# Where the PSUM pools of the attention stage lie: projections' pool at the far end, scores' pool ahead of the others

## The chip, the cores and the metric

One core of a Trainium2 chip runs the whole layer as one program. TensorE (PE in the profile) multiplies, VectorE (DVE), ScalarE (ACT) and GpSimd (POOL) do the rest, SyncE (SP) issues most DMAs. Results of TensorE land in PSUM, which the program sees as eight banks, each 512 float32 wide on 128 partitions. The metric is the device time of one execution in microseconds, lower is better; the figure for a kernel is the median of its runs.

## The reference

One layer of a hybrid encoder: 2048 tokens, width 1024, everything in float32.

```python
h = rmsnorm(x, norm_mix_g)
proj = h @ w_in                                  # 1024 -> 512 (ssm) + 3 * 512 (q, k, v)
y_ssm = s5_mixer(u_ssm, ...)                     # diagonal complex scan, GELU, then y * sigmoid(y @ w_glu + b_glu)
y_att = chunked_attention(q, k, v, rel_bias)     # chunks of 64 frames, 8 chunks to the left, 8 heads of 64
mixed = concat([rmsnorm(y_ssm), rmsnorm(y_att)])
x = x + mixed @ w_out
h2 = rmsnorm(x)
x = x + (silu(h2 @ w_gate) * (h2 @ w_up)) @ w_down
return rmsnorm(x)
```

## The kernel before

Float32 accuracy comes from splits: an operand is cut into a high half that the multiplier takes as it is (a ScalarE copy to the type fp32r) and a low half, the rest (a VectorE subtraction); `split` at line 179 does both, and a product of two split operands is three matmuls (`mm3`, line 173): high by high, high by low, low by high.

The stages follow each other on TensorE: the SSM's input projection (`u_phase`), the attention over four blocks of 512 tokens with q, k and v projections and the SSM scan woven in (`att_phase`), the mixing (`mix_phase`: the gate of the SSM's output, two RMS norms, the output projection), then the feed-forward part (`gate_up_phase`, `down_phase`). The attention goes by 128 steps: at each step a generator per unit of work is advanced by so many pieces, and the matmuls are kept in the order in which the Python code emits them (`Ordered`, line 76). Semaphore waits are put in by the framework: the first instruction that writes a new tile waits until the last readers and writers of whatever lay in that memory are done, as far as an earlier wait on the same engine hasn't covered it.

PSUM is dealt out in pools, taken from a stack that grows from bank 0, or with `side="right"` from bank 7:

- `apf` (line 1856), two banks, for the whole of the attention: the tiles `pf`, into which the projections, the gate's first products and the small norm products go.
- `ups`, `ups2`, later `apro`: the banks of the stages ahead of the attention.
- `aps` (line 1036): the transposed probabilities `pt` (two banks) and two tiles `pj` of one bank (the probabilities times v, and products of the SSM).
- `aps2` (line 1037): the scores `sc`, two banks.
- After the attention all eight banks become one pool of four tiles `big` of two banks each (`pp`, line 1828). By the built program they are dealt in the order banks 0 and 1, 6 and 7, 4 and 5, 2 and 3, and round again.

The end of the attention overlaps the start of the mixing. `mix_phase` (line 1124) is a generator of which 17 pieces (`MIX_N`) run in the last steps of the attention: the gate of block 0 (its products in `pf` tiles), the loads and splits of block 1's gate operand (`load`, line 1324, tiles `w` of the pool `lp`, one high and one low half for each of four row groups), and then

```python
pb = bank()                                  # a pf tile
spread(k, te, pb, b.o[0], 0)                 # four transposes put the norm factors into pb
rstd2(b, 0, pb[:])                           # four VectorE products ya <- ya * gain * pb, line 1243
...
for n, _ in enumerate(glu(nxt, bk)):         # block 1's gate: four output tiles of 12 matmuls
    if n == R1:
        rstd1(b, 1, bk())
```

`bk` (line 1330) gives `pf` tiles as long as the attention lasts and `big` tiles after it. In this kernel all four output tiles of block 1's gate come after the attention, so the first of them is the first `big` tile. VectorE runs strictly in its own order there: the splits of `w`, the first product on `pb`, the gate's products on `raw` (line 1226), sums of squares (line 1163), and, between them, the other three products on `pb`.

Behind the gate stand the halves of the output projection that need the attention's part alone (`mixed(b, 0)`, `w_out`), the norm of the SSM's part, and the rest. The output weights of rows 0 to 511 were split during the attention (`out_weights`) and come back as halves by DMA (`woh`, `wol` from `wos`); the other half is split here.

## Time and profile before

| what | value |
|---|---|
| three runs | 2203.41, 2207.74, 2212.28 us |
| median | 2207.74 us |
| the profiled execution | 2205.35 us, of which the span from first to last instruction is 2203.6 us |
| granted TensorE clock, mean over the span | 0.996 |
| TensorE busy | 2146.7 us, 97% of the span |
| VectorE busy | 1534.4 us, 70% |
| ScalarE busy | 1005.5 us, 46% |
| DMA | 439.59 MB, 199 GB/s over the span |

The profile is one execution. In its rows a time is microseconds from the span's start, then how long the row lasted, the engine, the source line, the operation, the tile written and the tiles read, the shape and how many instructions the row merges. In brackets stands how long the engine had been idle ahead of it and what ended the idle time. "PEclk" and the clock columns give the granted share of TensorE's full clock. A line such as L83 is that of a helper through which all matmuls go; the tile names tell which stage a row belongs to.

### The profile page before, as it was taken

Reading aid. Unit: us, or ns where it says so; the run is one execution under the profiler, and the core shown is the slowest. Engines: PE = TensorE matmul, PEld = TensorE weight load, DVE = VectorE, ACT = ScalarE, POOL = GpSimd, SP = SyncE. Lnnn points to the kernel's source line nnn. Section 1 sums busy time; section 2 is a strip of 40 time slices with the busy share of each in tenths; the row PEclk is TensorE's granted clock in tenths of the full one; section 3 lists DMA queues with packets and bytes.
Section 4 is the critical chain, followed back from the end, with each engine's and each line's share of the span. In section 5 each row is a group of like instructions: output and inputs, shape, how many; then the busy total and the mean of one; then the engine's idle time right before and its main releaser. Section 6 shows DMA issues by size and latency. Waiting matters only on the chain.

```text
span 2203.6 us, 30105 instructions
## 1 busy us (share of the span) xinstructions
PE 2146.7 (97%) x10606; PEld 1810.2 (82%) x10606; DVE 1534.4 (70%) x2671; ACT 1005.5 (46%) x1686; POOL 374.1 (17%) x839
## 2 busy tenths in 40 slices
PE   8999999999998999999999999999999999999998
PEld 7787898898886888788888887888888787888887
DVE  8767566665566667767766768766665577689785
ACT  6356566565576521633333344333333443354332
POOL 3367777676210000000000000000000100000000
PEclk9999999999999999999999999999999999999999
DMA  9788978966644347736555558555332495465552
GB/s 334 233 286 272 300 229 265 295 191 189 206 132 158 124 146 231 253 105 196 167 168 201 200 184 283 173 174 194 105 124 91 136 379 187 159 222 196 194 217 77
DMA packets 197879, 439.59 MB, mean 199 GB/s; under 512 B 20128, under 2 KB 37584, under 8 KB 190624
## 3 DMA queue, kind: packets, MB, share of 16 engines
q1 hardware_dynamic: 189904, 412.44, 56.1%
q0 software_dynamic: 7824, 25.24, 3.7%
q8 instruction: 83, 1.36, 0.2%
q14 instruction: 68, 0.56, 0.1%
HBM read 294.20 MB, written 135.29 MB: 195 GB/s over the span
## 4 chain that ended last, share of the span: by engine, by line
PE 80%; DVE 6%; DMA 5%; POOL 4%; issue 3%; ACT 2%; SPq 0%; DVEq 0%; ACTq 0%; POOLq 0%
PE X L83 21%; PE ps L83 20%; PE Y L83 11%; PE pf L83 8%; PE big L83 7%; PE W L83 5%; PE pj L83 3%; PE pt L86 2%; PE sc L83 2%; DVE lo L181 1%; POOL X L646 1%; POOL st L643 1%; POOL X L645 1%; DMA x<-xt 1%; POOL st L644 1%
## 5 line engine op out<-in xcount | busy, mean ns | idle before, releaser
L83 PE MATMUL X<-hi,c 128*128 128x512 f32 x1408 | 451.3, 391 | 7.7 <-DVE c L181 7.0
L83 PE MATMUL ps<-hd,hd 128*128 128x512 f32 (+1 forms) x1920 | 428.7, 384 | 3.8 <-DVE hd L181 2.0
L83 PEld LDWEIGHTS ps<-hd,hd 128*128 128x128 f32 x1920 | 353.2, 188 | 75.5 <-DVE hd L181 2.7
L83 PEld LDWEIGHTS X<-hi,c 128*128 128x128 f32 x1408 | 265.5, 189 | 64.1 <-DVE c L181 7.8
L83 PE MATMUL X<-lo,c 128*128 128x512 f32 x704 | 275.1, 391 | 0.0
L181 ACT CAST hd<-hd 128x1536 fp32r<-128x1536 f32 (+1 forms) x106 | 147.6, 1394 | 232.0 <-DMA hd<-hq 167.7
L83 PE MATMUL Y<-hi,c 128*128 128x512 f32 x704 | 225.0, 390 | 1.5 <-DVE u L1562 1.5
L181 DVE TENSOR_TENSOR hd<-hd 128x1536 fp32r<-128x1536 f32 (+1 forms) x106 | 174.1, 1644 | 37.3 <-ACT hd L181 36.5
L181 DVE TENSOR_TENSOR c<-S,c 128x512 fp32r<-128x512 f32 x176 | 121.0, 688 | 101.7 <-ACT c L181 101.5
L1666 POOL DMA_DIRECT2D hd<-hq x7 | 5.2, 747 | 1065.2 <-PE X L83 1053.0
L1558 ACT COPY u<-X 128x512 f32<-128x512 f32 x132 | 77.5, 588 | 198.4 <-PE X L83 198.4
L181 ACT CAST c<-S 128x512 fp32r<-128x512 f32 x176 | 109.5, 622 | 122.9 <-PE Y L83 61.8
L83 PE MATMUL big<-m,woh 128*128 128x512 f32 x512 | 158.9, 391 | 0.0
L1700 DVE TENSOR_TENSOR acc<-acc,ps 128x512 f32<-128x512 f32 x196 | 130.2, 682 | 39.4 <-PE ps L83 39.2
L83 PEld LDWEIGHTS Y<-hi,c 128*128 128x128 f32 x704 | 133.0, 189 | 29.7 <-DVE u L1562 1.9
L83 PEld LDWEIGHTS X<-lo,c 128*128 128x128 f32 x704 | 132.8, 189 | 27.5
L181 ACT CAST c<-raw 128x512 fp32r<-128x512 f32 x132 | 82.3, 623 | 147.8 <-PE Y L83 71.2
L83 PE MATMUL pf<-hi,w 128*128 128x512 f32 x416 | 147.4, 407 | 0.0
L83 PE MATMUL Y<-lo,c 128*128 128x512 f32 x352 | 137.4, 390 | 0.0
L980 DVE TENSOR_TENSOR ptl<-pt,pth 128x640 fp32r<-128x640 f32 (+3 forms) x152 | 98.1, 646 | 43.8 <-ACT pth L979 39.8
L979 ACT CAST pth<-pt 128x640 fp32r<-128x640 f32 (+3 forms) x152 | 83.8, 551 | 79.9 <-PE pt L86 74.3
L963 ACT ACTIVATE s<-s,mn 128x640 f32<-128x640 f32 (+4 forms) x128 | 98.0, 765 | 46.5 <-DVE mn L960 43.5
(486 smaller groups left out, 4258.1 us busy)
## 6 DMA issues: line engine op xcount, KB each, us to landing
w<-wss SPq DMA_DIRECT2D x36, 1024.0 KB, 6.5
hq<-g SPq DMA_DIRECT2D x140, 256.0 KB, 2.1
hd<-hq SPq DMA_DIRECT2D x35, 768.0 KB, 4.4
hd<-wc SPq DMA_DIRECT2D x35, 768.0 KB, 5.9
raw<-in_w_gate SPq DMA_DIRECT2D x44, 512.0 KB, 3.7
raw<-in_w_up SPq DMA_DIRECT2D x44, 512.0 KB, 4.1
wc<-px SPq DMA_DIRECT2D x66, 256.0 KB, 3.2
wss<-w SPq DMA_DIRECT2D x12, 1024.0 KB, 6.4
```

The lines of the kernel that those rows point to most:

```text
L83: return self.tc.keep_in_program_order(self.tc.nc.tensor.matmul(*a, **b))
L86: return self.tc.keep_in_program_order(self.tc.nc.tensor.transpose(*a, **b))
L181: return nc.scalar.copy(hi, raw), nc.vector.tensor_tensor(lo, raw, f32(hi), op=ALU.subtract)
L643: eng.tensor_tensor(t[:, :, :, :n], src, ar, op=ALU.mult)
L644: eng.tensor_tensor(t2[:, :, :, :n], src[:, ::-1], aw, op=ALU.mult)
L645: eng.tensor_tensor(dst, dst, t[:, :, :, :n], op=ALU.add)
L646: eng.tensor_tensor(dst, dst, t2[:, :, :, :n], op=ALU.add)
L963: nc.scalar.activation(s[:, :nk], s[:, :nk], AF.Exp, bias=mn[:], scale=-1.0, accum_out=sums[sb, pr][:, hh, qp : qp + 1])
L979: nc.scalar.copy(pth[:, a:b, qp, :], pt[:, a:b, :])
L980: k.low = nc.vector.tensor_tensor(ptl[:, a:b, qp, :], pt[:, a:b, :], f32(pth[:, a:b, qp, :]), op=ALU.subtract).ins
L1558: nc.scalar.copy(u[:], ps[:])
L1700: V.tensor_tensor(a, a, ps[:], op=ALU.add)
```

## The change

Two edits. The pools `aps` and `aps2` are opened in the other order, and `apf` is taken from the right-hand end.

```diff
@@ -1033,8 +1033,8 @@
         nbt = S["nba"], k.t(aa, "nbb", [P, 640])
         bias_corners(k, nbt[1])
         sp = tc.alloc_tile_pool(name="ssm", reuse_waits="tile", bufs=1)
+        psum2 = cx.enter_context(tc.tile_pool(name="aps2", bufs=1, space=bass.MemoryType.PSUM, reuse_waits="tile"))
         psum = cx.enter_context(tc.tile_pool(name="aps", bufs=1, space=bass.MemoryType.PSUM, reuse_waits="tile"))
-        psum2 = cx.enter_context(tc.tile_pool(name="aps2", bufs=1, space=bass.MemoryType.PSUM, reuse_waits="tile"))
         units = []
@@ -1853,7 +1853,7 @@
-            with tc.tile_pool(name="apf", bufs=2, space=bass.MemoryType.PSUM, reuse_waits="tile") as k.pfs:
+            with tc.tile_pool(name="apf", bufs=2, space=bass.MemoryType.PSUM, reuse_waits="tile", side="right") as k.pfs:
```

In the built program the banks are then these:

| pool and tile | banks before | banks now |
|---|---|---|
| `apf`: `pf` | 0, 1 | 6, 7 |
| `aps2`: `sc` | 6-7 | 0-1 |
| `aps`: `pt` | 2-3 | 2-3 |
| `aps`: `pj` | 4, 5 | 4, 5 |
| `ups`: `ps` | 2 to 5 | 0 to 3 |
| `ups2`: `pp` | 6, 7 | 4, 5 |
| `big`, in the order dealt | 0-1, 6-7, 4-5, 2-3 | 0-1, 6-7, 4-5, 2-3 |

No instruction is added, removed or moved on any engine; what differs is waits on TensorE. The first is at the first score tile of the attention, whose wait for earlier matmuls names an earlier one of them (transposes into the pool `apro`). The second is on TensorE at the end of the attention, at the first `big` tile (`big_8444`, first output tile of block 1's gate; `w` is the gate operand, `hi`, `lo`, `xt` the gate's weights; a name in square brackets is the semaphore waited for, that of VectorE or of TensorE itself):

```order
-L83 MATMUL big_8444<-w_7913,hi_1467_6615 128x512 [waits DVE_49,PE_49]
 L83 MATMUL big_8444<-w_7913,hi_1467_6615 128x512
+L83 MATMUL big_8444<-w_7913,hi_1467_6615 128x512 [waits DVE_49]
 L83 MATMUL big_8444<-w_7913,lo_1468_6616 128x512
-L83 MATMUL big_8444<-w_7913,hi_1516_6847 128x512 x2
+L83 MATMUL big_8444<-w_7913,hi_1516_6847 128x512
+L83 MATMUL big_8444<-w_7913,hi_1516_6847 128x512 [waits DVE_49]
```

The tile's first matmul waits for nothing now; its second, which reads the low half of the operand, waits for the split of that half, and so does every third matmul after it. Before, the first matmul waited for the fourth product on `pb` (`pb` lay in the same banks) and needed no wait of its own for the splits, which stand ahead of that product on VectorE. The same wait stands now on TensorE twelve matmuls later, at the second `big` tile (`big_8460`, second output tile of the same gate), which lies on banks 6 and 7:

```order
-L83 MATMUL big_8460<-w_7913,hi_1467_6615 128x512 x2
+L83 MATMUL big_8460<-w_7913,hi_1467_6615 128x512 [waits DVE_49,PE_49]
+L83 MATMUL big_8460<-w_7913,hi_1467_6615 128x512
 L83 MATMUL big_8460<-w_7913,lo_1468_6616 128x512
 L83 MATMUL big_8460<-w_7913,hi_1516_6847 128x512 x2
```

Everything behind it, on all engines, waits for what it waited for before.

## The prediction

> **What bounds the kernel now.** I read the page's head and its chain of waits first.

> ```profile
> span 2203.6 us, 30105 instructions
> PE 2146.7 (97%) x10606; PEld 1810.2 (82%) x10606; DVE 1534.4 (70%) x2671; ACT 1005.5 (46%) x1686; POOL 374.1 (17%) x839
> PE 80%; DVE 6%; DMA 5%; POOL 4%; issue 3%; ACT 2%; SPq 0%; DVEq 0%; ACTq 0%; POOLq 0%
> ```

> TensorE is busy 97% of the span and holds 80% of the chain that ended last. An edit of waits can pay only where TensorE stands still: 2203.6 − 2146.7 = 57 us in all. So next the waits of TensorE by the instruction waited for (total us, times, longest).

> ```profile
> PE pt L86 <- DVE ptl L980: 13.8, 18, 2.2
> PE X L83 <- DVE c L181: 7.0, 2, 3.5
> PE big L83 <- DVE ya L1243: 6.3, 1, 6.3
> ```

> The third line is the place of the change: one single wait of 6.3 us, for the products on `pb` at line 1243. TensorE's timeline around it:

> ```profile
> 673.00 0.62 PE L86 MATMUL pj<-ident,rb 128*128 128x128 f32 x4
> 679.96 1.19 PE L83 MATMUL big<-w,hi 128*128 128x512 f32 x2 [6.34 <-DVE ya L1243]
> 685.21 0.76 PE L83 MATMUL big<-w,hi 128*128 128x512 f32 x2
> 688.08 0.62 PE L83 MATMUL big<-w,hi 128*128 128x512 f32 x2
> 690.13 0.94 PE L83 MATMUL big<-ones,sq 128*128 128x1 f32 x8
> ```

> The last work of the attention ends at 673.62. The gate's first output tile starts at 679.96, its second at 685.21, its third at 688.08. Twelve matmuls take 685.21 − 679.96 = 5.25 us the first time; nine of the third tile take 690.13 − 688.08 = 2.05, so twelve are 2.73 us at their full pace. The first tile ran slowly, and the views by windows (columns: length, busy time and count of PE, PEld, DVE, ACT, POOL, then the granted clock, DMA share, GB/s) say why:

> ```profile
> 678.00:679.00 1.00, 0.00 (x0) 0.00 (x0) 1.00 (x2) 0.74 (x2) 0.00 (x0) 0.83 1.03 315
> 683.00:685.00 2.00, 2.00 (x6) 1.53 (x5) 0.73 (x2) 0.00 (x0) 0.00 (x0) 0.50 1.03 420
> 685.00:686.00 1.00, 1.00 (x4) 0.81 (x4) 0.00 (x0) 0.50 (x1) 0.00 (x0) 0.76 1.03 422
> ```

> The granted clock falls to half inside the gap (0.83 over 678 to 679: from about 678.66) and returns at about 685.48 (0.76 over 685 to 686). So the wait costs its 6.34 us and some 2.6 us of slow matmuls behind it.

> **The change, part by part.** The first edit that can show is at the first score tile, whose wait for earlier transposes now names an earlier one.

> ```profile
> 126.33 0.30 PE L83 MATMUL sc<-hi2x,hi0x 128*128 128x128 f32 x1
> ```

> That row has no idle time ahead of it, so nothing stood there to be saved, and an earlier event can't be later: 0.

> The second is the `big` tiles. The first one now lies where the scores lay; its own waits are the splits of `w`. VectorE's and ScalarE's rows:

> ```profile
> 670.47 2.49 DVE L181 TENSOR_TENSOR w<-w,w 128x512 fp32r<-128x512 f32 x4
> 679.07 0.74 DVE L1243 SCALAR_TENSOR_TENSOR ya<-ya,ga,pf 128x512 f32<-128x512 f32 x1
> 681.24 2.49 DVE L181 TENSOR_TENSOR m<-ya,m 128x512 fp32r<-128x512 f32 x4
> 679.84 0.62 ACT L181 CAST m<-ya 128x512 fp32r<-128x512 f32 x1 [0.64 <-DVE ya L1243]
> 685.50 0.69 ACT L1229 ACTIVATE sg<-big,bg 128x512 f32<-128x512 f32 x1 [5.04 <-PE big L83]
> 686.22 0.69 DVE L1230 TENSOR_TENSOR w<-w,sg 128x512 f32<-128x512 f32 x1 [2.50 <-ACT sg L1229]
> ```

> The four splits end at 672.96, ahead of 673.62, so the first tile runs at once: twelve matmuls, still at the full clock (it fell only at 678.66), 673.62 + 2.73 = 676.35. The second tile lies under `pb` and waits for the fourth product, which VectorE ends at 679.07 + 0.74 = 679.81. Nothing that VectorE does between 670.47 and there reads what TensorE writes after 673.62, so that time stays, and the second tile starts at 679.96, where the first one did. The gap shrinks from 6.34 to 679.96 − 676.35 = 3.61 us.

> What that is worth depends on the pace of the second tile. Before, 24 matmuls took 688.08 − 679.96 = 8.12 us from the end of the wait; now twelve are left. At full pace they take 2.73 us: gain 8.12 − 2.73 = 5.39. At the pace of the first tile before, 5.25: gain 2.87. Which one is read from the other two gaps of this length:

> ```profile
> 908.58 1.22 PE L83 MATMUL X<-hi,c 128*128 128x512 f32 x2 [3.51 <-DVE c L181]
> 907.00:908.00 1.00, 0.00 (x0) 0.00 (x0) 1.00 (x3) 0.00 (x0) 0.00 (x0) 0.67 1.01 391
> 914.00:915.00 1.00, 1.00 (x6) 0.82 (x5) 0.62 (x1) 1.00 (x3) 0.00 (x0) 0.91 1.24 377
> 1349.88 0.73 PE L83 MATMUL X<-hi,c 128*128 128x512 f32 x2 [3.46 <-DVE c L181]
> 1350.00:1352.00 2.00, 2.00 (x7) 1.58 (x8) 2.00 (x4) 0.00 (x0) 0.00 (x0) 0.77 0.00 0
> 1352.00:1354.00 2.00, 2.00 (x6) 1.56 (x5) 0.84 (x2) 0.44 (x1) 0.00 (x0) 0.50 0.64 217
> 1354.00:1355.00 1.00, 1.00 (x4) 0.79 (x4) 0.00 (x0) 0.67 (x2) 0.00 (x0) 0.76 0.83 311
> ```

> After an idle stretch of 3.51 us the clock was halved from about 907.34 to 914.18, which cost half of the 5.6 us that TensorE worked in it: 2.8 us. After 3.46 us it was halved for 0.92 + 2.00 + 0.48 = 3.4 us, from about 1351.1: 1.7 us lost. Both gaps are a little shorter than the 3.61 us to come, and both brought the clock down, so I take a fall. By a long fall the gain is 2.87, by a short one 8.12 − (2.73 + 1.7) = 3.69. Two of the three falls seen (678.66, 907.34) were long: (2 × 2.87 + 3.69) / 3 = 3.1 us.

> [...]

> **Does the gain reach the end?** Behind the second tile every wait must be met about 3 us sooner. ScalarE's sigmoid of the first tile can run at 680.46 (behind its cast at 679.84) in place of 685.50, and VectorE's product with it behind its `m` splits, at 681.24 + 2.49 = 683.73; both engines stood idle there for lack of the first tile (5.04 and 2.50 us), so their queues move up too. On TensorE the whole stretch behind is full, except for short waits for the norm's first step (`nv`) of 0.8 us in all:

> ```profile
> 690.00:735.00 45.00, 44.74 (x216) 37.45 (x215) 29.28 (x79) 21.99 (x33) 0.00 (x0) 1.00 0.43 142
> 735.00:780.00 45.00, 44.75 (x212) 37.40 (x212) 26.43 (x62) 28.30 (x38) 0.00 (x0) 1.00 0.39 127
> 850.00:910.00 60.00, 56.49 (x252) 46.52 (x251) 44.13 (x78) 23.16 (x37) 0.00 (x0) 0.98 0.80 261
> PE big L83 <- DVE nv L112: 0.8, 3, 0.3
> 709.39 1.28 ACT L1196 ACT_TABLE_LOAD   x1
> 710.69 4.20 ACT L1196 ACTIVATE raw<-yr 128x512 f32<-128x512 f32 x4
> L1175 SPq DMA_DIRECT2D yr<-y x4: 462/1088/3620, 690.0 to 694.8; - x4
> DMA to landing us min/median/max: 6.4/7.0/8.8
> ```

> Of the transfers, the one that doesn't hang on TensorE is `yr`: issued up to 694.8 and landed at the latest by 694.8 + 8.8 = 703.6 for a GELU that starts at 710.69. It has 7 us to spare. SyncE issues it behind loads that wait for the output weights' splits, which move up as well; even unmoved it would do. So I carry 3.1 us to the end: 2205.35 − 3.1 = 2202.2 for an execution like the profiled one. The three runs have their median 2.4 us above it, so I state 2207.74 − 3.1 = **2204.6 us**.

> **The rivals.**
> *The clock holds* through the shorter gap: 5.39 us, 2207.74 − 5.4 = 2202.3. [...] Against it: both gaps near 3.5 us fell. [...]

> *The gain is lost behind.* Between 850 and 910 TensorE waits once for 3.5 us, at 908.58, at the end of a chain of transfers, with DMA busy 0.80 of the time. If these are paced by the queues and not by TensorE, TensorE gets there 3 us sooner and waits 6.6: time 2207.7. Against it: that stretch's loads and stores are released by results of the output projection, which move with TensorE.

> *The banks themselves cost time.* The scores are now read from banks 0 and 1, next to the transposes in 2 and 3, and the projections go to 6 and 7. If reading or writing there were slower, the place is the score step:

> ```profile
> L960 DVE CUSTOM_DVE_ANT_0 s<-sc,nbb 128x640 f32<-128x640 f32 (+2 forms) x64 | 47.3, 739 | 39.5 <-PE sc L83 37.7 <-POOL st L643 1.2
> L83 PE MATMUL X<-lo,c 128*128 128x512 f32 x704 | 275.1, 391 | 0.0
> L83 PE MATMUL Y<-lo,c 128*128 128x512 f32 x352 | 137.4, 390 | 0.0
> L83 PE MATMUL W<-lo,c 128*128 128x512 f32 x176 | 68.5, 389 | 0.0
> ```

> The attention has 128 such steps; 0.1 us more on each, all of it exposed, is 12.8 us: 2207.7 − 3.1 + 12.8 = 2217.4. It outweighs the gain from 0.024 us a step on. Against it: in the built program `W` lies on banks 0 and 1, `X` on 2 to 4, `Y` on 5 to 7, and the same matmul takes 389, 391 and 390 ns.

> *Nothing changes* because the first tile waits for something that the profile hides behind the late product: 2207.7. I count it with the lost gain; the order of waits leaves only the splits, which end by 672.96.

> **How the numbers follow.** The forecast, clock fallen, gain kept: 0.6. Clock holds: 0.15. Gain lost or absent: 0.15. Banks slower: 0.1, by all sizes. A change under 0.5% (11 us) can't be told from none by measuring this kernel. The first three cases lie at 2202 to 2208, all inside it; only the slow-bank case crosses it upward, half of the time: slower 0.05. Faster by over 0.5% needs the full 5.4 us and another 5.6 from the spread of the runs (4.5 us on either side of the median): 0.04. Same: 0.91. The range takes the cases' ends, 2202.3 and 2207.7, and for the scatter of a median of few runs such as those shown about 4 us below and 3 above: 2198 to 2211.

> **What would show it.** In the changed profile TensorE's first `big` row should stand directly behind the last `pj` row with no idle time, last about 2.7 us for twelve matmuls, and be followed by one gap of 3.6 us ended by `ya` L1243; the second tile should run at a granted clock of 0.5 and the third start 2.9 to 3.7 us sooner after the end of the attention. The stretch from there to 850 should be as full as before, and the wait at `X` near 905 still about 3.5 us. A gap of 6 us at the first tile would say that the wait wasn't the one named; a longer wait at `X` would say that the gain was lost; longer L960 rows or fuller idle time in the attention would say that the banks matter.

## The result, and the profile after

The change ran 22 times beside 22 runs of the kernel before: median 2207.44 us (2199.93 to 2211.37) against 2210.88 (2203.41 to 2218.30). The ratio is 0.9981, 95% interval 0.9973 to 0.9989: 2210.88 × 0.0019 = 4.2 us faster, 2.4 to 6.0. Forecast were 3.1 us and 2204.6 us. The time lies 2.8 us above that because the kernel before, run 19 times more, has its median 3.1 us above the three runs shown; by size and sign the difference is as forecast. The prediction held that a change under 11 us can't be told from none; with 22 runs on each side 4.2 us can.

The waits of TensorE in the changed kernel (total us, times, longest), three lines of the list:

```profile
PE X L83 <- DVE c L181: 6.5, 2, 3.4
PE big L83 <- DVE ya L1243: 3.6, 1, 3.6
PE pj L83 <- DMA Bst<-bsts: 2.5, 1, 2.5
```

The wait at `big` went from 6.3 to 3.6 us. TensorE's timeline at the place, end of the attention to third tile of the gate:

```profile
680.80 0.62 PE L86 MATMUL pj<-ident,rb 128*128 128x128 f32 x4
681.18 0.71 PE L83 MATMUL big<-w,hi 128*128 128x512 f32 x2
...
683.32 0.84 PE L83 MATMUL big<-w,xt 128*128 128x512 f32 x3
687.78 0.70 PE L83 MATMUL big<-w,hi 128*128 128x512 f32 x2 [3.62 <-DVE ya L1243]
...
692.19 0.63 PE L83 MATMUL big<-w,hi 128*128 128x512 f32 x2
```

The first tile stands directly behind the attention, without idle time; the wait now stands ahead of the second. From the end of the attention (680.80 + 0.62 = 681.42) the third tile starts 692.19 − 681.42 = 10.77 us later; before it was 688.08 − 673.62 = 14.46. That is 3.69 us. VectorE and ScalarE there:

```profile
678.30 2.49 DVE L181 TENSOR_TENSOR w<-w,w 128x512 fp32r<-128x512 f32 x4
686.89 0.75 DVE L1243 SCALAR_TENSOR_TENSOR ya<-ya,ga,pf 128x512 f32<-128x512 f32 x1
688.32 0.69 ACT L1229 ACTIVATE sg<-big,bg 128x512 f32<-128x512 f32 x1
```

The fourth product ends at 687.64, 6.22 us after the end of the attention, as before (679.81 − 673.62 = 6.19). The first sigmoid runs as soon as ScalarE is free, 6.90 us after that end in place of 11.88. The clock behind the gap, by windows (granted clock is the third number from the right):

```profile
688.00:689.00 1.00, 1.00 (x5) 0.77 (x5) 0.90 (x2) 0.97 (x3) 0.00 (x0) 0.84 1.05 418
689.00:692.00 3.00, 3.00 (x9) 2.32 (x8) 3.00 (x6) 1.89 (x3) 0.59 (x1) 0.50 1.02 408
692.00:693.00 1.00, 1.00 (x6) 0.82 (x5) 1.00 (x2) 0.81 (x2) 0.00 (x0) 0.96 1.06 426
```

It was halved for 0.32 + 3.0 + 0.08 = 3.4 us: a short fall, 1.7 us lost, and by the prediction's own sum 8.12 − (2.73 + 1.7) = 3.69 us gained.

The profiled execution itself is longer than that of before, 2209.6 against 2203.6 us, and that has nothing to do with the place: the attention ended 7.8 us later (681.42 against 673.62). The third wait above, for a transfer at 202.04, is one part of it, 2.5 us. Slow clock at two other places is another:

```profile
260.00:267.00 7.00, 6.00 (x25) 5.26 (x26) 1.51 (x2) 4.48 (x11) 4.13 (x9) 0.76 1.00 395
507.00:515.00 8.00, 6.29 (x20) 5.38 (x21) 4.23 (x8) 2.54 (x5) 5.75 (x8) 0.57 0.90 257
```

At half the clock these cost up to 7 × (1 − 0.76) = 1.7 and 8 × (1 − 0.57) = 3.4 us. The kernel before shows a scatter of that size without the change: the mean granted clock is 0.989 to 0.996 in its five profiles and 0.993 here. Two single spans can't be compared to a few microseconds here. The distance between two landmarks around the place can, and the ratio over many runs.

### The profile page after: what moved, and what is told of

It reads as the page before. It is cut to its first block, busy times and chain, and to the rows that moved or that the text cites. A ratio compares the mean times of both kernels' runs of the same rounds, so it can differ in the third digit from the quotient of the medians.

```text
span 2209.6 us, 30105 instructions
## 1 busy us (share of the span) xinstructions
PE 2153.8 (97%) x10606; PEld 1815.0 (82%) x10606; DVE 1535.5 (69%) x2671; ACT 1004.9 (45%) x1686; POOL 372.7 (17%) x839
## 4 chain that ended last, share of the span: by engine, by line
PE 80%; DVE 6%; DMA 5%; POOL 4%; issue 3%; ACT 2%; SPq 0%; DVEq 0%; ACTq 0%; POOLq 0%
PE ps L83 21%; PE X L83 20%; PE Y L83 10%; PE pf L83 8%; PE big L83 7%; PE W L83 5%; PE pj L83 3%; PE pt L86 2%; PE sc L83 2%; DMA lo<-hc 1%; DVE lo L181 1%; POOL X L646 1%; DMA x<-xt 1%; POOL X L645 1%; DMA raw<-in_w_out 1%
## 5 line engine op out<-in xcount | busy, mean ns | idle before, releaser
L83 PE MATMUL X<-hi,c 128*128 128x512 f32 x1408 | 450.6, 391 | 7.2 <-DVE c L181 6.5
L83 PE MATMUL ps<-hd,hd 128*128 128x512 f32 (+1 forms) x1920 | 430.1, 385 | 2.0 <-DVE hd L181 2.0
L83 PEld LDWEIGHTS ps<-hd,hd 128*128 128x128 f32 x1920 | 354.4, 189 | 74.0 <-DVE hd L181 2.7
L83 PEld LDWEIGHTS X<-hi,c 128*128 128x128 f32 x1408 | 265.1, 188 | 63.5 <-DVE c L181 7.3
L83 PE MATMUL X<-lo,c 128*128 128x512 f32 x704 | 274.6, 390 | 0.0
L181 ACT CAST hd<-hd 128x1536 fp32r<-128x1536 f32 (+1 forms) x106 | 147.5, 1394 | 232.3 <-DMA hd<-hq 166.8
L83 PE MATMUL Y<-hi,c 128*128 128x512 f32 x704 | 225.1, 390 | 1.9 <-DVE u L1562 1.5
L181 DVE TENSOR_TENSOR hd<-hd 128x1536 fp32r<-128x1536 f32 (+1 forms) x106 | 174.2, 1644 | 37.0 <-ACT hd L181 36.5
L181 DVE TENSOR_TENSOR c<-S,c 128x512 fp32r<-128x512 f32 x176 | 121.0, 688 | 100.7 <-ACT c L181 100.5
L181 ACT CAST c<-S 128x512 fp32r<-128x512 f32 x176 | 109.5, 622 | 122.0 <-PE Y L83 62.1
L83 PE MATMUL big<-m,woh 128*128 128x512 f32 x512 | 161.2, 396 | 0.0
L83 PEld LDWEIGHTS Y<-hi,c 128*128 128x128 f32 x704 | 132.5, 188 | 30.6 <-DVE u L1562 2.4
L83 PEld LDWEIGHTS X<-lo,c 128*128 128x128 f32 x704 | 132.6, 188 | 27.6
L181 ACT CAST c<-raw 128x512 fp32r<-128x512 f32 x132 | 82.2, 623 | 147.7 <-PE Y L83 70.7
L83 PE MATMUL pf<-hi,w 128*128 128x512 f32 x416 | 148.8, 410 | 0.0
L83 PE MATMUL Y<-lo,c 128*128 128x512 f32 x352 | 137.2, 390 | 0.0
L980 DVE TENSOR_TENSOR ptl<-pt,pth 128x640 fp32r<-128x640 f32 (+3 forms) x152 | 98.1, 646 | 43.9 <-ACT pth L979 39.8
```

Source lines behind the costliest of these rows:

```text
L83: return self.tc.keep_in_program_order(self.tc.nc.tensor.matmul(*a, **b))
L181: return nc.scalar.copy(hi, raw), nc.vector.tensor_tensor(lo, raw, f32(hi), op=ALU.subtract)
L980: k.low = nc.vector.tensor_tensor(ptl[:, a:b, qp, :], pt[:, a:b, :], f32(pth[:, a:b, qp, :]), op=ALU.subtract).ins
```

## The experiments

Twelve runs followed, of eight kernels: the kernel before and the change again, and six others. The table gives for each the distance from the end of the attention to the start of the gate's third tile and to the four transposes of the SSM norm (`big<-ident,no`, the last landmark ahead of the norm's product), from one profile each, and the ratio to the kernel before with its interval. The kernel before has five profiles; its distances to the third tile were 14.46, 14.57, 14.79, 13.66 and 13.96 us, mean 14.29, and to the transposes 31.74, 31.85, 32.07, 30.93 and 31.24 us, mean 31.57.

| kernel | third tile, us | transposes, us | ratio | interval |
|---|---|---|---|---|
| before | 14.46 | 31.74 | 1 | |
| the change | 10.77 | 28.09 | 0.9981 | 0.9973 to 0.9989 |
| the change again | 10.69 | 28.07 | 0.9987 | 0.9976 to 0.9998 |
| far end only | 10.77 | 28.09 | 0.9988 | 0.9977 to 0.9999 |
| scores first only | 13.27 | 30.55 | 1.0000 | 0.9988 to 1.0013 |
| first tile twice | 9.16 | 26.43 | 0.9974 | 0.9962 to 0.9986 |
| products early, far end | 5.32 | 24.48 | 0.9973 | 0.9961 to 0.9984 |
| products early, old banks | 9.28 | 26.56 | 0.9962 | 0.9946 to 0.9977 |
| first tile eight times | 24.36 | 41.64 | 1.0048 | 1.0031 to 1.0064 |

**One edit at a time.** Far end only:

```diff
-            with tc.tile_pool(name="apf", bufs=2, space=bass.MemoryType.PSUM, reuse_waits="tile") as k.pfs:
+            with tc.tile_pool(name="apf", bufs=2, space=bass.MemoryType.PSUM, reuse_waits="tile", side="right") as k.pfs:
```

> Only the pool pf goes to the far end; the transposes pt then lie on banks 0-1, pj on 2 and 3, the scores on 4-5. Theory (a wait of TensorE for the late product on pb, and the clock behind it): the first big tile lies under pt, long read, so it starts at once as in the change, and the second waits for the product. From the end of the attention's last matmul to the start of the gate's third tile 9.1 us if the clock holds, 10.8 after a short fall, 11.6 after a long one (14.5 before); ratio to before about 0.998, between 0.9975 and 0.9988. Rival (the place of the scores' banks carries part of the gain): less than that, nearer to 1.000.

Scores first only is the other half of the diff, `aps2` opened ahead of `aps`.

> Only the scores' pool is opened first: sc on banks 2-3, pt on 4-5, pj on 6 and 7, pf stays on 0 and 1. Theory: the first big tile still lies under pf, TensorE waits 6.3 us there for the product at line 1243, 14.5 us to the third tile; ratio 1.000, within 0.001. Rival (banks have a speed of their own): three pools of the attention have moved, so the score and transpose rows get longer or shorter and the ratio leaves 1.000 by more than 0.001.

In TensorE's timelines, the far end alone has the changed kernel's picture, a first tile at once and 3.6 us ahead of the second:

```profile
676.17 0.62 PE L86 MATMUL pj<-ident,rb 128*128 128x128 f32 x4
676.55 0.71 PE L83 MATMUL big<-w,hi 128*128 128x512 f32 x2
683.14 0.70 PE L83 MATMUL big<-w,hi 128*128 128x512 f32 x2 [3.59 <-DVE ya L1243]
687.56 0.63 PE L83 MATMUL big<-w,hi 128*128 128x512 f32 x2
```

and the scores' order alone has that of before:

```profile
675.48 0.62 PE L86 MATMUL pj<-ident,rb 128*128 128x128 f32 x4
682.46 1.19 PE L83 MATMUL big<-w,hi 128*128 128x512 f32 x2 [6.35 <-DVE ya L1243]
```

So the edit on `apf` is the change; opening the scores' pool first adds nothing that these runs can tell. That its third tile comes at 13.27 us, ahead of all five profiles of before, lies in the clock: it came back 9.3 us after the end of the attention, in those five 10.1 to 12.5 us after it. The kernel with the scores first alone moves the scores, the transposed probabilities and `pj` to other banks and its time is the same, 1.0000. The score rows of the changed kernel, in the list of costliest groups, are as long as before (739 ns):

```profile
L960 DVE CUSTOM_DVE_ANT_0 s<-sc,nbb 128x640 f32<-128x640 f32 (+2 forms) x64 | 47.3, 739 | 42.4 <-PE sc L83 41.8
```

The rival that the banks have a speed of their own is out for these three pools, to within the interval of 0.0012. For the banks of the change itself the traces say the same: its attention, with the kernels built on it, ends at 674.8 to 681.4 us in four profiles, that of the kernel before at 673.6 to 679.7 in five.

**The clock behind the gap.** The second pass over the first tile fills most of the gap with work:

```diff
-                for q in range(4):
-                    mm3(te, ps[:, :512], Wg[q][0][:, cs], Wg[q][1][:, cs], *gate_operand(k, q), q == 0, q == 3)
+                for q in range(8 if f == 0 and twice else 4):
+                    mm3(te, ps[:, :512], Wg[q % 4][0][:, cs], Wg[q % 4][1][:, cs], *gate_operand(k, q % 4), q % 4 == 0, q % 4 == 3)
```

> The change, and the first output tile of block 1's gate is computed twice over (12 matmuls more; the second pass begins the sum anew), which fills 2.7 of the 3.6 us of the gap. Theory (the slow matmuls behind the gap come from the clock, which falls for idle time): gap 0.9 us, clock stays at 1.0, second tile in 2.7 us, third tile 9.1 us after the end of the attention; ratio 0.9975, so 1.7 to 2.5 us better than the change although it does more. Rival (the second tile is slow for another reason, the transfers that fill the DMA queues at that time): it takes 4.4 to 5.2 us again and the ratio is 0.998 to 0.9987.

```profile
683.99 0.70 PE L83 MATMUL big<-w,hi 128*128 128x512 f32 x2 [0.88 <-DVE ya L1243]
686.80 0.62 PE L83 MATMUL big<-w,hi 128*128 128x512 f32 x2
```

```profile
684.00:687.00 3.00, 3.00 (x13) 2.51 (x14) 2.90 (x5) 3.00 (x4) 0.59 (x1) 1.00 1.01 370
```

The second tile takes 686.80 − 683.99 = 2.81 us at a granted clock of 1.0 (second fence, by windows), while the DMA queues are as full as before (share 1.01). It isn't the transfers that slow the matmuls, it is the clock, and the clock stays up when the gap is short. A kernel that does twelve useless matmuls more reaches the third tile 1.6 us sooner than the change.

**The other end of the same wait.** Here the four products are put ahead of the gate's products on VectorE, once with the far end alone and once with the banks of before:

```diff
         for f in range(4):
-            load(nxt, f)
+            lo = load(nxt, f)
         pb = bank()
         spread(k, te, pb, b.o[0], 0)
-        rstd2(b, 0, pb[:])
+        with tc.issue_after(lo), tc.high_priority():
+            rstd2(b, 0, pb[:])
```

where `load` now returns its VectorE instruction.

> The far-end edit alone, and the four products on pb are put straight behind the splits of w on VectorE, ahead of the gate's products on raw. Theory (TensorE waits for VectorE's order alone): the fourth product ends about 3.9 us sooner, ahead of the first tile's end, so no wait is left at the second tile, the third starts 5.5 us after the end of the attention (14.5 before, 10.8 in the change's profile), no fall of the clock there. Some 2 us come back as waits for VectorE's halves of the output weights; net 6 to 7 us, ratio 0.997. Rival (what is won at this place is lost behind it): the third tile starts as early, but the time to the end is no better than the change's, ratio 0.998 or more.

> The banks as before the change, and the four products on pb straight behind the splits of w on VectorE, ahead of the gate's products on raw. Theory (the 6.3 us were a wait for VectorE's order, and a layout is only one way round it): the product ends about 3.9 us sooner, the first tile's gap is 2.3 to 2.5 us instead of 6.3, likely without a fall of the clock there; two tiles run through, the third starts 7.8 to 8.3 us after the end of the attention (14.5 before); ratio 0.9972 (0.996 to 0.9985). Rival (a first tile on pf's banks costs something beside the product): the gap stays over 4 us or the ratio is over 0.9985.

TensorE with the far end:

```profile
676.06 0.62 PE L86 MATMUL pj<-ident,rb 128*128 128x128 f32 x4
676.44 0.71 PE L83 MATMUL big<-w,hi 128*128 128x512 f32 x2
679.28 0.62 PE L83 MATMUL big<-w,hi 128*128 128x512 f32 x2
682.00 0.62 PE L83 MATMUL big<-w,hi 128*128 128x512 f32 x2
...
691.39 0.50 PE L83 MATMUL big<-m,wol 128*128 128x512 f32 x1 [0.52 <-DVE wol L181]
692.60 0.50 PE L83 MATMUL big<-m,wol 128*128 128x512 f32 x1 [0.24 <-DVE wol L181]
```

Three tiles run without a gap. What is won at the third tile, 14.46 − 5.32 = 9.14 us, is 31.74 − 24.48 = 7.26 at the transposes: VectorE is now late with the halves of the output weights (`wol`), the next wait in line, and the rest went in short waits and slower starts between. With the old banks a gap of 2.14 us is left ahead of the first tile:

```profile
677.85 0.70 PE L83 MATMUL big<-w,hi 128*128 128x512 f32 x2 [2.14 <-DVE ya L1243]
```

Against what was expected, this gap too brought the clock down, for 3.4 us, in this profile and in a second one (third tile at 9.28 and 9.27 us; expected were 7.8 to 8.3 without a fall). The ratio of 0.9962 is even better than its distances say, 5.2 us of 8.4, with an interval that reaches down to 5.1. The excess goes with the clock at other places: over its eight runs the mean granted clock is 0.9946, over the 21 of the kernel before beside them 0.9924, and 0.0022 of 2205 us is 4.9 us. Why this kernel had fewer falls there stays open.

Both kernels are ahead of the change where they ran in one series with its edit on `apf`: products early, far end, has a median of 2205.53 us against 2209.45 for the far end alone, and products early, old banks, 2202.68 against 2209.09 for the change again, with five of its eight runs below all twelve of the other (lowest 2204.29). Which of the two is faster isn't settled: their intervals overlap (0.9961 to 0.9984 and 0.9946 to 0.9977).

**Is time at this place carried to the end?** The same edit as for the second pass with 32 in place of 8.

> The change, and the first output tile of block 1's gate computed eight times over (84 matmuls more, each pass begins the sum anew), so that TensorE has no gap and the third tile starts 8 x 2.73 + 2.73 - 0.24 = 24.3 us after the end of the attention, 9.9 us later than before. Theory (time at this place is carried to the end one for one): ratio 1.0045, between 1.003 and 1.006. Rival (slack behind it, in the stretch of transfers from 850 to 910, takes up part of a shift): 1.001 to 1.003, and the wait at X near 910 gets shorter by as much.

The third tile came 24.36 us after the attention and the transposes 41.64 − 31.74 = 9.9 us later than before; the time rose by 0.0048 × 2212 = 10.6 us (6.9 to 14.2). One for one within the interval. The wait at `X` near the end of the mixing is still 3.6 us, as before:

```profile
PE X L83 <- DVE c L181: 3.6, 1, 3.6
```

**The change and the kernel before, again.** In the traces of the kernel before and of the change the falls of the clock stand whole steps of 3.41 us apart: 67 and 130 steps between those at 678.65, 907.34 and 1351.08 us of the one, 72, 53, 12 and 16 between those at 262.01, 507.77, 688.68, 729.64 and 784.25 us of the other. Up to the last fall, at the end of the span, the clock comes back after 3.41 us, one step, or 6.83, two. These steps are the grid of the expectations.

> The change itself once more, beside the others. Theory: the third tile starts 9.1 (clock holds), 10.8 (short fall) or 11.6 us (long fall) after the end of the attention; a fall is likelier; ratio 0.998. The two falls of the clock near 730 and 784, each without an idle stretch of more than 0.3 us, stand in its first profile: if they belong to the moved banks they are there again, if they hang on where the grid of the clock's steps lies they may be or not.

> The kernel before, once more, for a second profile. Theory: gap of 6.3 us, third tile 13.3 to 14.5 us after the end of the attention. Falls of the clock near 726, 781 and 842, which all five profiles with moved banks show and the one of before does not: if the banks cause them they are absent again; if the grid does, they may be there.

The change showed a short fall once more (third tile at 10.69 us). Two falls of the clock without an idle stretch, which its first profile has at 730 and 784, were there again too, at 726 and 781, and the kernel before had none. By then seven profiles of moved banks showed one or more such falls (the kernel with the first tile eight times one alone, behind an idle stretch of 1.47 us) and three of old banks none. Four more profiles of old banks bear on this.

> The kernel before, one more profile, for the falls of the clock near 46 and 100 us after the end of the attention (two 1-column products of the norm stand there), which all seven profiles with moved banks have at one or both places and three with the old banks have not. By the built program the tiles in use there lie on the same banks in all of them. Theory (where the grid of the clock's steps lies against those products decides): some of the four looks of this call show such a fall. Rival (the moved banks bring it): none does.

> As e10, another execution of the kernel before: under the theory a fall near 46 or 100 us after the end of the attention in about every second look; under the rival none.

> As e10, another execution of the kernel before: under the theory a fall near 46 or 100 us after the end of the attention in about every second look; under the rival none.

> The old banks with the products on pb put early (e6), another execution: its gap of 2.1 us brought the clock down once; theory: it does so where the gap lies within one step of the grid, so it may or may not here, and the third tile starts 9.3 us (fall) or 7.6 us (none) after the end of the attention. Falls near 44 and 97 us after the end: as for e10.

Of the three profiles of the kernel before, one had a fall at 784 and 846, one at 729 and 784, one none; the fourth kernel had all three, at 724, 779 and 840. The one at 729, by windows:

```profile
728.00:729.00 1.00, 1.00 (x6) 0.84 (x5) 1.00 (x9) 0.28 (x1) 0.00 (x0) 0.97 0.77 211
729.00:732.00 3.00, 3.00 (x9) 2.33 (x8) 3.00 (x23) 0.35 (x2) 0.00 (x0) 0.50 0.72 270
```

The old banks have them as well, so the moved banks aren't their cause. The gap of 2.14 us of the fourth kernel, 677.87 to 680.01, brought the clock down once more; by windows (0.51 over 680 to 683, 0.77 over 683 to 684) it fell at about 680.06, so the gap lay whole inside the step of 3.41 us ahead of the fall.

What goes with a fall in the mixing can be read from the traces of the kernel before and of the change. The edges of the steps lie differently in the two: the first one behind the end of the attention comes 1.62 us after it in the one and 0.43 us in the other. At the full clock 15 matmuls of 512 columns fill a step (12 take 2.73 us). Two groups of eight 1-column products take about 2 us, so a step that holds both has room for few others: for the fall at 729 it was the step from 725.5 to 728.9, with the columns of 5.3 such matmuls. In each of the two traces two groups stand close together at three places of the mixing. The emptiest step there held 9.1, 5.4 and 9.4 such matmuls in the kernel before, and the clock fell behind none of them; in the change it held 5.2, 4.4 and 6.5, and the clock fell behind the first two (729.64 and 784.25).

## Why the prediction was right

The time alone would not have shown it: 2207.44 us lies nearer to the rival in which the gain is lost (2207.7) than to the forecast (2204.6), and the range of 2198 to 2211 holds the times of both and that of the clock that holds (2202.3). What tells them apart is the ratio to the kernel before, run beside it, and the distances in the traces.

*The place and the wait.* The change takes away the wait at the first tile and puts it ahead of the second, 3.62 us long against the 3.61 forecast. That the wait is one for VectorE's order, and not for the banks as such, is shown twice: the scores' pool alone leaves it as it was, and the products put early shorten it with the old banks.

*The release doesn't move.* The fourth product ends 6.22 us after the attention's end against 6.19.

*The pace behind the gap* was the uncertain term, with 2.87 to 5.39 us between its ends. All three profiles with this gap (the change twice, the far end alone) show a short fall and the third tile at 10.7 to 10.8 us, thus a gain of 3.7 us against the one profile of before that the sum was made on. Against the mean of five profiles of the kernel before the gain at the transposes is 31.57 − 28.08 = 3.5 us. The forecast of 3.1 weighted two long falls against one short; the size is 0.4 to 0.6 us off, its sign and case are right.

What goes with a long or a short fall can be read from the traces of the kernel before and of the change. Behind the first 12 us and up to its last matmul TensorE stood idle for over 3.3 us five times (6.34, 3.51 and 3.46 us in the one, 3.62 and 3.43 in the other), and each time the clock fell. Of the stretches of 2 to 3.3 us, two of 2.16 us in the change brought it down (at 262.01 and 507.77), those of 2.51 and 3.02 us there and one of 2.16 in the kernel before did not. Of these seven falls four came 0.9 to 1.3 us ahead of the end of the stretch, and they lasted 6.83 us (678.65 and 907.34; 507.77 and 1354.28); three came 0.9 to 1.2 us behind it, and they lasted 3.41 (1351.08; 262.01 and 688.68). In the three profiles with this gap the clock fell 0.8 to 1.1 us behind its end. As that moment differs from execution to execution, three short falls of three are in part luck.

The rival in which the clock holds did not occur in three of three; with the gap cut to 0.88 us it did hold. In the one profile that the forecast was made on, the clock held through the gap of 2.16 us at `pt` (granted 1.00 from 500 to 507); in the change's profile it fell at the same gap (granted 0.50 from 508 to 514).

*Carried to the end.* Gains and losses at the place, from 9.9 us lost to 7.3 us gained at the transposes, are found in the time of the whole within the intervals; the rival that the stretch of transfers takes them up is out for a loss of 9.9 us, where it would have shown as a shorter wait at `X`. For the change alone, 3.5 us lies inside both its intervals (2.4 to 6.0, and 0.4 to 5.3 us in the repeat), which are too wide to exclude a loss of one microsecond on the way. The traces exclude it up to `X`: from the end of the attention to the start of the idle stretch at `X` near 910, less 1.7 us for each fall of the clock between the transposes and there, it is 230.5 to 231.6 us in the five profiles of before (mean 231.2) and 227.5 to 227.6 in the three with this gap, 3.6 us less; and the stretch itself, 3.0 to 3.7 us there, is no longer than the 2.8 to 3.9 of before. It is over 4 us only with the products early and the far end, 4.3, so part of that kernel's gain may be lost there.

*The banks* cost nothing that can be measured: with three pools moved the ratio is 1.0000, and the score rows of the changed kernel take 739 ns as before, as the equal rows of `W`, `X` and `Y` (389, 391 and 390 ns) had said.

## What to carry to other kernels

Where PSUM changes hands between two stages, list for each bank the last reader in the old stage and give the banks that are read last to the tile that is written last in the new one: the wait doesn't vanish, but work slides in ahead of it (here the twelve matmuls of one tile, and 6.34 us became 3.62). Look at the late reader as well: moving four products ahead of work that nobody was waiting for shortened the same gap from 6.3 to 2.1 us without touching the banks, and gained more. Count a gap of TensorE with the slow matmuls that follow it (1.7 us lost behind 3.62 here), and measure an edit of a few microseconds by the distance of two landmarks in the trace, since two spans of one and the same kernel differed by 13.7 us.

## What the runs showed of the hardware

The granted clock goes with a good part of the scatter between executions. Five profiles of the kernel before, span and mean granted clock of the core:

```profile
core 0: 2203.6 us, clock 0.996
core 0: 2210.6 us, clock 0.994
core 0: 2208.7 us, clock 0.993
core 0: 2212.6 us, clock 0.992
core 0: 2217.3 us, clock 0.989
```

The share of the clock that wasn't granted, times the span, is 8.8, 13.3, 15.5, 17.7 and 24.4 us; the spans less these are 2194.8, 2197.3, 2193.2, 2194.9 and 2192.9. The spread of 13.7 us shrinks to 4.4. Over the 35 runs of this kernel in one series it shrinks less, from 11.7 to 9.1 us, and the standard deviation from 3.3 to 2.2.

The clock fell for less than the gaps of 3.46 us and more behind which the prediction saw it fall: after gaps of 2.14 us in both profiles of one kernel, and with no gap over 0.26 us where two groups of eight 1-column products stand close together, as here in a profile of the kernel before, ahead of the fall at 729:

```profile
725.56 0.94 PE L83 MATMUL big<-ones,sq 128*128 128x1 f32 x8
726.76 1.05 PE L83 MATMUL big<-ones,sq 128*128 128x1 f32 x8 [0.25 <-DVE nv L112]
```

Each such fall lasts about 3.4 us and costs 1.7; up to three of them stand in the mixing, and filling that place with wider matmuls wasn't tried.
